# A hybrid decoder layer: half boundaries on other banks, two diagonal score steps in one slot, casting copies moved off the sequence change, later loads at the start, and the last weights in a slot of their own

## The chip, the cores and the metric

One Trainium2 chip, all 8 cores. Each core computes two of the sixteen sequences and exchanges nothing with the others. The metric is the device time of the slowest core in microseconds. Some executions fall into a slower state, in which one die or both get a lower TensorE clock (in the slow run of `b_bank` 0.88 to 0.89 on cores 0 to 3 and 0.99 on the others, in one of `spread_model` 0.81 to 0.83 on all eight); they are named slow below and never compared with fast ones. Spans of single cores come from the profiled execution of each kernel.

## The reference, cut to what matters

```python
BATCH, SEQ, D_MODEL, D_FF = 16, 2048, 1024, 2816
# per layer (depth 1):
x = x + 0.5 * rms(swiglu(rms(x, g1), w_gate, w_up, w_down), g2)      # FFN 1
x = x + rms(hybrid_mixer(rms(x, g3)), g4)                            # attention
x = x + 0.5 * rms(swiglu(rms(x, g5), w_gate2, w_up2, w_down2), g6)   # FFN 2
# hybrid_mixer: one input projection (1024 -> 3072); 4 differential heads
# (two 64-wide score maps each, causal, dense, values 128 wide) beside
# 8 dilated heads (three window patterns); one output projection (1024 -> 1024)
```

## The kernel before

The program is one stream of nodes. A planner orders them for each engine at build time, with estimated durations; the chip then runs that fixed order, each engine waiting on semaphores. An FFN half is 1024 tokens of one sequence: a gate/up pass (22 jobs) and a down pass (8 jobs). Each job is done in seven products over sums of blocks instead of eight over the blocks themselves; banks `y` and `y + 1` take over the first product, which is needed twice, and accumulate others on top.

```python
DMA_RATE = 280.0          # what the planner assumes of transfers: GB/s, us, us
DMA_LAT = 2.4
DMA_AHEAD = 5.0
...
# gate/up pass
    y = (2, 6)[ji % 2]
    pb = (0, 4, y, 0, 4, y, y)[n]                   # bank of product n of job ji
    ...
    if n == 0:
        copy(two(y), [B_ps[y], B_ps[y + 1]], 0)     # banks 0,1 -> y,y+1 on ScalarE
...
# down pass
    y = 2 + ji % 2
    pb = (0, 4, y, 0, 4, y, y)[n]
...
# ffn_half: the normalisation of the half before is finished in banks 6 and 7
for k, p in enumerate(pend):
    p(6 + k, g.clock + 3.0 + 0.3 * k)
```

The second FFN's weights are cast from 32 to 16 bits by 30 copies from memory to memory, which run during attention. Attention goes through 16 units (8 head groups of two sequences). In the first step of each unit two copies are released, by the last TensorE node before them; four semaphores rotate, so at most four are under way:

```python
def cast_chunk(i, pace):
    ...
    g.dma(POOL, [(d, s_)], [pace], [b, B_ctr[i % 4]], kb * 1.15, track=B_ctr[i % 4])
...
for w, (s, u) in enumerate(units):
    ...
        if first:
            first = False
            ...                      # pace: written by the last TensorE node
            for c in range(2):
                if 2 * w + c < NF + NKC:
                    cast_chunk(2 * w + c, pace)
```

The units from the last of the first sequence to the first of the second are called the sequence change here. A differential score step computes one block of 128 keys against 512 queries, for two maps; on the diagonal only the later 512, 384, 256 or 128 queries count:

```python
def scores(Q, kt, box):
    mp = kt - 4 * Q
    c0 = max(mp, 0) * 128
    si = nxt("S", 2)                                # one of two pairs of banks
    ...                                             # 2 matmuls of 512 - c0 columns, 64 rows
    g.op([(ACT, a_ps(n), act_(P[:, :, c0:TT], sp[:, :, c0:TT], AF.Exp, ...))], bs, [bP])
...
for kt in range(4 * Q + 4):
    ...                                             # scores, then values, of step kt
```

The start loads the first input tile and weights, then the tile after and the next half's as soon as their buffers allow. At the very end, the second half of the last down pass takes its last weights through the ring of slots, and every square of the last statistics is added on VectorE before one product with ones on TensorE.

The softmax here doesn't subtract the row's maximum and nothing guards it: scores larger than these inputs give would overflow.

## Time and profile before

| | us |
|---|---|
| median of 3 runs (one of them slow, 2854.82) | 2540.53 |
| fast runs | 2539.59, 2540.53 |
| TensorE busy on core 4 (span 2536.5) | 2437.88 |

The view of the cores lists span and mean granted clock. Cores 6 and 7 were granted a lower clock in this execution and lose it in the first stage (189 and 192 us), the others lie within 15 us of each other:

```profile
core 2: 2524.9 us, clock 0.994
...
core 4: 2536.5 us, clock 0.993
...
core 7: 2562.1 us, clock 0.983
```

TensorE is busy nearly all the time, so the rows of engines say little. To see where time goes I divide each core's span at fixed matmuls of the program: the first down projection, the first value projection of attention, the first and the 256th matmul of the output projection (between them lies the sequence change), the first matmul of FFN 2, the last gate/up matmul and the last matmul of all. All stage tables below are worked out from the traces in this way and give the median over the 8 cores. For the kernel before:

| start | rest of FFN 1 | attention, first half | sequence change | attention, rest | FFN 2 to the last gate/up | last down pass | tail |
|---|---|---|---|---|---|---|---|
| 169.7 | 673.2 | 380.6 | 85.8 | 392.0 | 745.8 | 74.8 | 9.8 |

### The profile page before, as it was taken

How to read it: one execution, taken by the hardware profiler on the slowest of the kernel's cores; microseconds unless marked ns; L12 is line 12 of the kernel's file. 1: busy time of each engine (PE TensorE's matmuls, PEld its weight loads, DVE VectorE, ACT ScalarE, POOL GpSimd, SP SyncE). 2: the span in 40 equal slices, each digit the busy share in tenths (PEclk: the TensorE clock that was granted, in tenths of full speed). 3: DMA queues.
4: the chain of work that ended last, by engine and by line, in shares of the span. 5: the costliest groups of instructions: out<-in, count | busy, mean ns of one | idle time of the engine just before them, and what ended most of it. 6: DMA issues, size and time to landing. Idle time of an engine off the chain costs nothing.

```text
span 2562.1 us, 49653 instructions; the slowest of 8 cores (2521.7 to 2562.1 us)
## 1 busy us (share of the span) xinstructions
PE 2465.2 (96%) x16526; PEld 1289.4 (50%) x16526; DVE 1854.5 (72%) x3172; ACT 1398.7 (55%) x2070; POOL 421.7 (16%) x483
## 2 busy tenths in 40 slices
PE   6999999999999999999989999999999999999997
PEld 4444444444444556656546666544444444444466
DVE  6656796797797774556687455499777967967974
ACT  4433654554554477777677677775434544534433
POOL 1110220121131221111122110013102101201302
PEclk9889999999999999999999999999999999999999
DMA  7565586496596993425569352258245444534634
GB/s 172 112 132 132 146 167 135 141 185 115 148 203 117 221 207 70 64 55 122 118 152 219 84 100 40 58 171 255 90 135 168 144 132 156 167 122 137 201 124 143
DMA packets 154969, 356.15 MB, mean 139 GB/s; under 512 B 28416, under 2 KB 39296, under 8 KB 154112
## 3 DMA queue, kind: packets, MB, share of 16 engines
q1 hardware_dynamic: 129872, 260.89, 33.7%
q0 software_dynamic: 24848, 92.09, 22.5%
q8 instruction: 138, 2.26, 0.4%
q14 instruction: 111, 0.91, 0.1%
HBM read 381.84 MB, written 80.48 MB: 180 GB/s over the span
## 4 chain that ended last, share of the span: by engine, by line
PE 89%; DVE 3%; ACT 2%; issue 2%; DMA 2%; POOL 0%; DVEq 0%; ACTq 0%; POOLq 0%; SPq 0%
PE ps L942 41%; PE ps L1011 21%; PE ps L1147 8%; PE ps L1278 5%; PE ps L1109 4%; PE ps L1184 3%; PE ps L1243 3%; PE ps L1407 2%; ACT M L641 2%; DVE M L638 1%; PE ps L1370 1%; DMA M<-xT 1%; DMA M<-x 1%; DVE M L770 0%; DVE M L704 0%
## 5 line engine op out<-in xcount | busy, mean ns | idle before, releaser
L641 ACT ACTIVATE M<-ps 128x1024 bf16<-128x1024 f32 (+8 forms) x1191 | 880.7, 777 | 578.2 <-PE ps L942 174.8
L942 PE MATMUL ps<-M 128*128 128x512 f16 (+1 forms) x5096 | 1101.1, 379 | 22.9 <-ACT ps L641 10.6
L638 DVE TENSOR_TENSOR M<-M 128x1024 f16<-128x1024 f16 (+10 forms) x1602 | 953.1, 629 | 222.2 <-ACT M L641 95.5
L942 PEld LDWEIGHTS ps<-M 128*128 128x128 f16 x5096 | 503.7, 99 | 614.8 <-issue 105.4
L641 ACT ACTIVATE M<-M 128x512 f32<-128x512 f32 (+4 forms) x648 | 385.9, 618 | 490.9 <-DVE M L638 417.8
L1011 PE MATMUL ps<-M 128*128 128x512 f16 (+2 forms) x2926 | 547.6, 348 | 4.0 <-DMA M<-cdn 2.5
L638 POOL TENSOR_TENSOR M<-M 128x512 f32<-128x512 f32 (+3 forms) x248 | 305.9, 1240 | 1277.7 <-DVE M L770 570.5
L1011 PEld LDWEIGHTS ps<-M 128*128 128x128 f16 x2926 | 276.1, 99 | 269.3 <-issue 21.9
L638 DVE TENSOR_TENSOR M<-ps,M 128x1024 f32<-128x1024 f32 (+5 forms) x322 | 304.2, 948 | 129.5 <-PE ps L1011 72.6
L1147 PE MATMUL ps<-M 128*128 128x512 f16 x1024 | 263.0, 379 | 4.7 <-DVE M L1121 1.8
L638 DVE TENSOR_TENSOR M<-M,ps 128x512 f16<-128x512 f32 (+1 forms) x182 | 120.9, 665 | 64.7 <-PE ps L942 44.8
L1278 PE MATMUL ps<-M 128*128 128x129 bf16 x2176 | 162.8, 221 | 1.9 <-DVE M L638 1.7
L1278 PEld LDWEIGHTS ps<-M 128*128 128x128 bf16 x2176 | 134.2, 98 | 47.9 <-issue 26.3
L1109 PE MATMUL ps<-M 128*128 128x128 f16 x2048 | 141.3, 219 | 8.3 <-DVE M L1307 2.4
L704 DVE SCALAR_TENSOR_TENSOR M<-M,gains 128x512 f16<-128x512 f32 x192 | 134.9, 748 | 16.8 <-ACT M L641 16.6
L641 ACT ACTIVATE ps<-ps 128x1024 f32<-128x1024 f32 (+3 forms) x129 | 108.2, 839 | 62.7 <-PE ps L1011 45.1
L770 DVE SCALAR_TENSOR_TENSOR M<-M,gains 128x512 f16<-128x512 f16 x176 | 140.0, 815 | 1.6 <-ACT M L641 1.5
L1109 PEld LDWEIGHTS ps<-M 128*128 128x128 f16 x2048 | 119.8, 98 | 27.1 <-issue 22.5
L1147 PEld LDWEIGHTS ps<-M 128*128 128x128 f16 x1024 | 86.1, 97 | 86.5 <-issue 23.7
L1184 PE MATMUL ps<-M 128*128 128x512 f16 x512 | 119.5, 382 | 8.5 <-DVE M L1094 5.8
L1094 DVE CAST M<-ps 128x512 bf16<-128x512 f32 (+1 forms) x97 | 66.9, 689 | 76.1 <-PE ps L1147 56.2
L1243 PE MATMUL ps<-M 64*128 64x512 bf16 (+3 forms) x640 | 96.3, 352 | 10.3 <-ACT M L641 10.0
(54 smaller groups left out, 750.1 us busy)
## 6 DMA issues: line engine op xcount, KB each, us to landing
M<-x SPq DMA_DIRECT2D x128, 512.0 KB, 6.5
M<-cgu SPq DMA_DIRECT2D x88, 512.0 KB, 4.2
M<-xT SPq DMA_DIRECT2D x64, 512.0 KB, 8.1
x<-M SPq DMA_DIRECT2D x64, 512.0 KB, 7.2
M<-wgu POOLq DMA_DIRECT2D x58, 512.0 KB, 8.4
M<-cdn SPq DMA_DIRECT2D x38, 704.0 KB, 4.3
M<-wd POOLq DMA_DIRECT2D x32, 704.0 KB, 8.0
M<-c1g SPq DMA_DIRECT2D x30, 512.0 KB, 4.2
```

What stands on the lines that cost most here:

```text
L638: return lambda e: e.tensor_tensor(o, a, b, op)
L641: return lambda e: e.activation(o, i, f, **k)
L704: g.op([(DVE, v_stt(512), lambda e, o=o, kc=kc: e.scalar_tensor_tensor(o, halves(xt.ap(kc)), gains[:, gcol + kc:gcol + kc + 1], halves(rst ...
L770: g.op([(DVE, v_stt(512), lambda e, y=y, d=d: e.scalar_tensor_tensor(y, y, gains[:, gcol + d:gcol + d + 1], rst[ri], ALU.mult, ALU.mult))] ...
L942: g.pe([(lambda e, gg=gg, kc=kc, pb=pb, src=src, piece=piece, n=n, w=w, cs=cs: e.matmul(bank(pb + gg)[:, 0:w], src[:, gg * 512 + kc * 128: ...
L1011: g.pe([(lambda e, k=k, b=pb, src=src, piece=piece, n=n, c0=c0, W_=W_: e.matmul(bank(b)[:, 0:W_], src[:, k * 128:(k + 1) * 128], H[piece][ ...
L1094: g.op([(DVE, vc or v_ps(n), lambda e: e.tensor_copy(o, i)), (ACT, a_ps(n), act_(o, i, AF.Copy))], rd, wr, pen=EVPEN)
L1109: g.pe([(lambda e, kc=kc: e.matmul(bank(pb)[:, tq * 128:(tq + 1) * 128], xn[:, kc, t * 128:(t + 1) * 128], wap[:, kc * 128:(kc + 1) * 128] ...
L1147: g.pe([(lambda e, kc=kc: e.matmul(bank(pb), wap[:, kc * 128:(kc + 1) * 128], xn[:, kc, ts(tt)], start=(kc == 0), stop=(kc == NKC - 1)), [ ...
L1184: g.pe([(lambda e, k=k: e.matmul(bank(pb), wap[:, k * 128:(k + 1) * 128], mixT[k][:, ts(tt)], start=(k == 0), stop=(k == NKC - 1)), [wb, B ...
L1243: g.pe([(lambda e, m=m: e.matmul(sp[:, m, c0:TT], KT[i][64 * m:64 * m + 64, kt * 128:(kt + 1) * 128], QT[i][64 * m:64 * m + 64, Q * TT + c ...
L1278: ops.append((lambda e, a_ap=a_ap, m=m, uq=uq, first=first: e.matmul(a_ap, P[:, m, uq * 128:(uq + 1) * 128], Vt[i][:, kt, 0:129], start=(k ...
```

## The change

Five parts. The half boundaries of the FFN change banks, so that the first copy of a half needs no bank that the down pass still holds. Diagonal score steps 1 and 3 share a slot. Casting copies avoid the first unit and the sequence change, and others take up to three. The start gates some loads, chains others behind the second input tile, and gives the planner slower transfers. At the end the last weights get their own slot and the last squares go straight to TensorE. The matmuls multiply as much as before.

```diff
-DMA_RATE = 280.0
-DMA_LAT = 2.4
-DMA_AHEAD = 5.0
+DMA_RATE = 260.0
+DMA_LAT = 3.0
+DMA_AHEAD = 8.0
...
+OWN = 2
+NXH = 2
+CHAIN = 2
...
+CASTS = (0, 2, 3, 2, 3, 2, 2, 0, 0, 2, 3, 3, 3, 3, 2, 0)
...
-                y = (2, 6)[ji % 2]
+                y = (6, 2)[ji % 2]
...
+                        elif lead and l < lead + CHAIN:
+                            b = x1[0]
+                            aft = [[b.buf(3)], [b.buf(5)]] if l == lead else [[W[l - 1][k][1]] for k in (0, 6)]
+                            W[l] = load_blocks(fi, "g", l, after=aft)
...
+                def parts(Q, kt):
+                    r = [(kt, max(kt - 4 * Q, 0) * 128, max(kt - 4 * Q, 0) * 128)]
+                    if kt == 4 * Q + 1:
+                        r.append((kt + 2, 384, 0))
+                    return r
...
-                    for kt in range(4 * Q + 4):
+                    for kt in range(4 * Q + 3):
...
-                        for c in range(2):
-                            if 2 * w + c < NF + NKC:
-                                cast_chunk(2 * w + c, pace)
+                        for c in range(CASTS[w]):
+                            cast_chunk(sum(CASTS[:w]) + c, pace)
...
-                p(6 + k, g.clock + 3.0 + 0.3 * k)
+                p(2 + k, g.clock + 3.0 + 0.3 * k)
...
-                                 c + 20.0 + 20 * tl)
+                                 c + 20.0 + 20 * tl, after=[B_H[0][NXH]] if (s, fi, h) == (0, 0, 0) else ())
...
+                wx = (o_RS, rbuf("wx", o_RS, 5632))
...
-                sa, sb_ = Stat(3, 256), Stat(2, 256)
+                sa = Stat(3, 256, own=[(ssum[i], B_ssum[i]) for i in range(OWN)])
+                sb_ = Stat(2, 256, own=[(sq[i], B_sq[i]) for i in range(OWN)])
...
-                               (2, (1,), 0, 128, fa), (1, (1,), 128, 128, fb), (2, (1,), 128, 128, fb)], keep, {3: W[3]})
+                               (2, (1,), 0, 128, fa), (1, (1,), 128, 128, fb), (2, (1,), 128, 128, fb)], keep, {3: W[3]},
+                          {2: lambda kind, j: wx if j == 0 else ring_slot(kind, j)})
```

## The prediction

Where a cut is marked, statements that no trace of this case shows were taken out; the figures left between the cuts were read from the trace of the kernel before. The sum came to 26 us.

> **What bounds the kernel now.** I read the table of cores first, then the busy time of each engine in stretches of 50 us, then who the tensor engine waited for, then the timeline around its longest waits. The page is of core 7, whose clock was granted lower (0.983); I read core 4 instead, which spans 2536.5 us at a clock of 0.993, close to the timed median of 2540.5 us. From the stretches of core 4 (columns: stretch, its length, busy us of each engine with instruction counts, granted clock, DMA share, GB/s):
>
> ```profile
> 0.00:50.00 50.00, 27.79 (x185) 18.66 (x185) 29.19 (x56) 21.52 (x38) 5.84 (x13) 0.90 0.78 169
> 50.00:100.00 50.00, 45.03 (x289) 27.81 (x290) 40.51 (x80) 27.46 (x51) 9.83 (x14) 1.00 0.69 121
> ...
> 850.00:900.00 50.00, 47.20 (x514) 30.94 (x513) 42.22 (x82) 35.36 (x55) 12.75 (x16) 1.00 0.86 168
> ...
> 1300.00:1350.00 50.00, 41.19 (x429) 25.34 (x427) 39.50 (x77) 33.31 (x51) 16.47 (x20) 0.97 0.87 200
> ...
> 1600.00:1650.00 50.00, 43.94 (x398) 24.23 (x397) 28.56 (x60) 37.67 (x53) 2.33 (x2) 0.93 0.13 42
> ...
> 2500.00:2550.00 50.00, 21.75 (x326) 20.10 (x324) 14.31 (x43) 11.69 (x37) 9.62 (x14) 0.85 0.33 108
> ```
>
> The sum of that table gives TensorE 2437.88 us busy of 2536.5, so all idle time together is 98.6 us. No other engine is near: VectorE is busy 1855 us, ScalarE 1397. The change removes no matrix multiplication, so it can gain only from those 98.6 us, from matmuls run at a lower clock, and from small gaps inside busy stretches. By stage the idle is: 27 us before 100, about 9 in the first FFN from 100 to 845, 46 in attention (845 to 1706), 5 in the second FFN, and some 15 after 2500. The waits of TensorE on core 4 (us in total, times, longest):
>
> ```profile
> PE ps L942 <- ACT ps L641: 11.3, 9, 1.9
> PE ps L731 <- DVE M L638: 11.0, 1, 11.0
> PE ps L1243 <- ACT M L641: 10.0, 18, 1.1
> ...
> PE ps L1184 <- DVE M L1094: 6.6, 5, 5.3
> ...
> PE ps L1011 <- DMA M<-cdn: 2.0, 1, 2.0
> ```
>
> The first is repeated at the FFN half boundaries, the fourth is one event at the sequence change, the fifth is the late weights of the end. The second is the wait for the first input tile; nothing in the change touches it. The timeline of one half boundary:
>
> ```profile
> 238.95 1.89 PE L942 MATMUL ps<-M 128*128 128x512 f16 x8
> ...
> 243.36 0.60 ACT L641 ACTIVATE M<-ps 128x512 f16<-128x512 f32 x1 [3.17 <-PE ps L1011]
> 244.11 1.15 ACT L641 ACTIVATE M<-M 128x512 bf16<-128x512 f16 x2
> ...
> 245.16 1.00 ACT L641 ACTIVATE ps<-ps 128x1024 f32<-128x1024 f32 x1
> ...
> 246.31 1.02 PE L942 MATMUL ps<-M 128*128 128x512 f16 x4 [1.37 <-ACT ps L641]
> ```
>
> The reader is to see that the first products of the new half were done at 240.8, but the copy of them from banks 0 and 1 to banks 2 and 3 started only at 245.16: bank 3 was the last accumulator of the down pass, freed by the 243.36 copy, and two squares ran in between. TensorE then stood 1.37 us. The sequence change, first from the chain of work in order of time, then the timeline:
>
> ```profile
> 1286.37 15.77 DMA M<-x
> ```
>
> ```profile
> 1279.87 0.98 POOL L147 DMA_DIRECT2D cgu<-wgu  x2 [12.82 <-PE ps L1278]
> ...
> 1302.35 3.25 POOL L638 TENSOR_TENSOR M<-M 128x512 f32<-128x512 f32 x3 [9.26 <-DMA M<-x]
> ...
> 1305.70 0.69 DVE L1311 TENSOR_REDUCE sml<-M 128x4 f32<-128x512 f32 x1 [5.75 <-POOL M L638]
> ...
> 1308.53 3.38 PE L1184 MATMUL ps<-M 128*128 128x512 f16 x8 [5.30 <-DVE M L1094]
> ```
>
> Two casting copies start at 1279.87; the residual load issued at 1286.37 takes 15.77 us; GpSimd's adds wait for it, VectorE's reduction waits for a GpSimd product queued behind them, the evacuation queued behind that is late, and TensorE stands 5.30 us.
>
> [...] 15.77 us against a median of 6.3 for these loads. [...] after 5.30 us of idle, 8 matmuls took 3.38 us against 1.89 for the same 8 elsewhere. [...] The groups by shape give 1022 ns for 1024 columns, 809 for 768 and 379 for 256, so fusing the last two saves 809 + 379 - 1022 = 166 ns.
>
> **The change part by part.**
>
> (1) Half boundaries. The FFN's jobs start on banks 6 and 7 instead of 2 and 3, which the down pass does not use, and the deferred statistics move to 2 and 3. The copy can then follow its matmuls at once, behind one matmul group of 1.7 us. Between 240 and 840 and between 1730 and 2450 the waits table gives three such waits each, 4.1 us each: 8.2 us in all. The last job of most halves now ends on banks 6 and 7 and meets no bank of the down pass. I take 8.
>
> (2) Casting copies. None in the first unit and in the units either side of the sequence change; others take 3. It removes the 5.30 us wait and the slow restart (3.38 - 1.89 = 1.5): 6.8. At the attention's start two waits of 0.86 and 0.81 us stand beside the first copies (issued at 872.8): I give 1. The same 30 copies remain and all still precede the second FFN. I take 7 in all, with something lost to other loads left there.
>
> (3) Diagonal scores. Steps 1 and 3 (384 and 128 columns) share one slot, so each query block has one step fewer: 4 blocks x 4 units x 2 sequences = 32 fewer of 320. Multiplications are as many. What goes is a change to 64-row mode and back. In the timeline at 1610.21, two 512-column matmuls (0.216 us each, from 126.91 us for 588 in the chain) end at 1610.64, the score group starts at 1610.73, its two pairs end at 1611.16 and the next starts at 1611.27: 0.09 + 0.11 = 0.2 us for a group. I counted 211 score groups on the timeline, 1.52 steps in each; 288 steps make 190, so 21 x 0.2 = 4.2 us. ScalarE saves 0.166 us in 8 steps, 1.3 us, beside other work. Against it: the shared step holds its banks through two activations in three heads of four, so the next one waits longer. I take 3.5.
>
> (4) Start. Loads for the next half wait until the third job has finished, the fourth and fifth weights wait for the second input tile, and the planner's transfer model is slower (260 instead of 280, latency 3.0 instead of 2.4). This should stop ScalarE from standing in program order behind squares whose input has not arrived: the 1.9 us at 65.31 and part of the 2.98 us at 38.02 and of the waits of about 1.4 nearby. I take 3.5.
>
> (5) End. The last weights have a slot of their own: 2.01 us of wait, and the restart at 2509.51 (11 matmuls of 128 columns in 1.23 us against 0.77 for 11 at 2523.80) gives 0.5. The last two squares go to TensorE directly: the final sum stood 1.92 us behind VectorE; two additions drop out, but only the last, 0.36 us with its hand-over, and its wait on the addition before are on the chain, say 0.8. VectorE may share the last additions without penalty (0.37 us each against GpSimd's 0.7): say 0.7. I take 4.
>
> Sum: 8 + 7 + 3.5 + 3.5 + 4 = 26 us.
>
> **The rivals.** First, a new static order. The program is ordered by a planner at build time; the altered transfer model and slots shift thousands of instructions, and some of the 46 us of attention idle comes back elsewhere. For it: its waits are many and small (18 on score banks, 10.0 us). Against it: the planner had these same rules before. It would make 2520 to 2530. Second, the sequence change may stay bound by transfers: output weights and residual tiles load there as well (DMA share 0.87 from 1300 to 1350), so only half of the 6.8 us returns, and units with three copies instead of two see late loads: 2520. Third, the fewer steps and the calmer transfers help more of the attention than I count, perhaps 10 us of its 46: 2503. Fourth, ScalarE becomes the bound in attention; it is busy there about three quarters of the time, and the change takes a little from it, so I give this little.
>
> **Range and chances.** 2540.5 - 26 = 2514.5; I say 2515, 1.0% less. Eight in ten: 2503 (all parts whole, attention a little better) to 2529 (boundaries and end alone). Faster by over 2% means below 2489.7, 51 us of the 98.6, while some 11 at the start and much of the last 15 can't go: 3%. Slower by over 2% needs a serious new wait: 1%. Within 2%: 96%.
>
> **What would show it.** (1) The waits of about 1.4 us on the copies at the six half boundaries are gone. (2) The 5.30 us wait is gone and residual loads there land in 6 to 9 us. (3) 288 score steps, some 190 groups, and attention shorter by 10 us or so with (2). (4) Idle before 100 us falls from 27 to about 23. (5) No wait for the last weights; the stretch after 2500 shorter by 4. The prediction fails if idle in attention grows elsewhere by over 10 us, or if the FFN loses less than 6 us.

## More of the kernel before

The sequence change has two values: 88 to 91 us on cores 0, 3, 4 and 7, 82 to 84 on the others. Attention as a whole takes 858.7 in the median.

## The result, and the profile after

| | before | after |
|---|---|---|
| median of 4 runs each, same chip | 2540.06 (one slow) | 2527.45 (2526.12 to 2528.03) |
| ratio of fast runs, 95% interval | | 0.9953 (0.9933 to 0.9972) |

A ratio here is the mean time of one kernel's fast runs over that of the other's of the same rounds, so it is not quite the ratio of the medians quoted. The gain is some 12 us where 25 were predicted. By stage, in us:

| | start | FFN 1 rest | att. first half | seq. change | att. rest | FFN 2 | last down | tail | attention, whole |
|---|---|---|---|---|---|---|---|---|---|
| before | 169.7 | 673.2 | 380.6 | 85.8 | 392.0 | 745.8 | 74.8 | 9.8 | 858.7 |
| after | 170.6 | 667.7 | 383.1 | 83.5 | 394.2 | 738.9 | 70.3 | 9.7 | 860.4 |
| predicted change | -3.5 | -4.1 | with the rest | about -7 | -10.5 in all of attention | -4.1 | -4 with the tail | | -10.5 |

Both FFNs and the end gained more than was said or as much; the start and attention, 14 us of the predicted 26, gained nothing. The cores of the changed kernel tell more. The view of the cores, after:

```profile
core 0: 2523.2 us, clock 0.990
core 1: 2524.6 us, clock 0.990
core 2: 2508.7 us, clock 0.993
```

Core 2 is 15 us shorter than its neighbours with the same program, and its mean clock is higher. Whatever costs the others 15 us is not in the order of instructions. The waits of TensorE on core 0 after (us in total, times, longest; L752 is the first statistics, which wait for the first input tile, L968 the gate/up products, L1135 the value projection, L1173 the query and key projection):

```profile
PE ps L752 <- DVE M L650: 13.0, 1, 13.0
...
PE ps L1173 <- DVE M L1120: 6.1, 4, 2.9
PE ps L1135 <- issue: 5.8, 2, 4.7
...
PE ps L1173 <- issue: 2.5, 1, 2.5
```

Two things are to be seen. The waits of the gate/up products on ScalarE's copies, 11.3 us on core 4 before, have left the top of the list, and between 240 and 835 us, and again between 1730 and 2440, this view lists no wait at all. And a new kind has come: "issue", a wait for nothing that the profile shows. Before, all waits of that kind came to 0 to 1.9 us on a core; after, to 8.3, 10.6, 0.6, 9.7, 3.4, 6.1, 6.1 and 8.6 us on cores 0 to 7. The core with 0.6 is the short one. (In later kernels that keep the old placing of the copies, two at a time, these waits come to up to 4.1 us on a core, in `a_nocast` to 6.0: they are not new in kind, but in size.)

The half boundary that the prediction showed, in the timeline of core 0 after:

```profile
239.40 1.89 PE L968 MATMUL ps<-M 128*128 128x512 f16 x8
...
241.13 2.54 PE L1037 MATMUL ps<-M 128*128 128x512 f16 x11
241.39 1.01 ACT L653 ACTIVATE ps<-ps 128x1024 f32<-128x1024 f32 x1 [0.74 <-PE ps L968]
...
243.50 3.83 PE L968 MATMUL ps<-M 128*128 128x512 f16 x17
```

The copy from bank to bank starts 0.1 us after its matmuls end, not 4 us later, and TensorE goes from one group to the next without a bracket, that is without a wait.

The stretches of 50 us, core 0 after (columns as in the prediction):

```profile
0.00:50.00 50.00, 25.16 (x156) 16.61 (x157) 29.32 (x56) 21.66 (x37) 5.14 (x12) 0.84 0.71 148
50.00:100.00 50.00, 49.56 (x319) 31.83 (x318) 37.77 (x74) 26.35 (x49) 9.56 (x14) 0.95 0.74 141
...
1300.00:1350.00 50.00, 44.94 (x494) 29.42 (x493) 44.29 (x82) 36.19 (x53) 15.11 (x17) 0.98 0.83 207
...
1600.00:1650.00 50.00, 45.02 (x420) 24.94 (x420) 30.95 (x64) 39.12 (x55) 2.33 (x2) 0.97 0.19 54
2500.00:2550.00 50.00, 11.47 (x189) 10.63 (x186) 10.90 (x31) 6.67 (x21) 9.25 (x13) 0.91 0.16 45
```

TensorE of this core is busy 25.16 + 49.56 = 74.7 us of the first 100, where core 4 of the kernel before was busy 27.79 + 45.03 = 72.8, so that idle time seems to have fallen by 1.9. Yet it had done 156 + 319 = 475 matmuls by 100 us, and before 185 + 289 = 474. The busy time that seems gained is slower time: the granted clock is 0.84 and 0.95 where it was 0.90 and 1.00. This is why busy time alone can't be read as progress. These are two different cores, too, and core 4, with 27.2, had the most idle time of the eight before: the median of the cores is 24.9 us of idle in the first 100 in both kernels. The sequence change (1300 to 1350) has 494 matmuls in 50 us instead of 429: that part of the change did what it was for. On all cores: before, TensorE stood 6.3, 3.8, 5.3 and 4.4 us there on cores 0, 3, 4 and 7, and the residual loads around it landed in 4.8 to 16.8 us; after, no core stands over 2 us before the output projection there, and these loads land in 3.6 to 6.1 us.

At the end, the chain of work of core 4 before went through a transfer of 8.56 us to the last weights; that of core 0 after shows one unbroken piece of down projection in its place:

```profile
2500.81 8.56 DMA M<-cdn
```

```profile
2484.39 17.93 PE ps L1037 x242
```

**The new waits.** The longest of them in the timeline of core 0, GpSimd and TensorE (L147 is the helper that issues copies):

```profile
1474.52 1.01 POOL L147 DMA_DIRECT2D cdn<-wd  x2 [1.41 <-PE ps L1135]
...
1479.95 0.55 POOL L147 DMA_DIRECT2D cdn<-wd  x1
...
1485.57 0.40 PE L1135 MATMUL ps<-M 128*128 128x128 f16 x4
...
1490.67 1.46 PE L1135 MATMUL ps<-M 128*128 128x128 f16 x12 [4.70 <-issue]
```

A burst of three casting copies is issued, and some 6 us after the last one TensorE stops for 4.70 us in the middle of one group of sixteen matmuls, which need nothing new. Core 2 at the same instruction:

```profile
1482.73 0.84 PE L1135 MATMUL ps<-M 128*128 128x128 f16 x12 [0.59 <-issue]
```

So the place in the program is the same and the length differs by core. The transfers of core 0 after, from 1466.06 to 1487.6 us, as the view of the queues lists them (packets, MB, share of the 16 engines; then KB and us to landing for an issue):

```profile
q0 software_dynamic: 661, 2.95, 94.3%
q14 instruction: 1, 0.01, 0.1%
...
cdn<-wd POOLq DMA_DIRECT2D x3, 704.0 KB, 15.2
M<-win POOLq DMA_DIRECT2D x3, 256.0 KB, 4.7
```

(Queue q0 carries the copies, `cdn<-wd`, and loads of projection weights, `M<-win`: three of 704 KB and three of 256 KB make up its 2.95 MB. The last of these loads was issued at 1472.58, before the copies, and these loads land in 4.7 us.)

Queue q8, which the profile also calls "instruction", is not in the list. Its packets in the trace are of 16,384 bytes each; they end at 1450.3, 1457.3 and 1466.06, then there is none until one runs from 1487.61 to 1489.16, and TensorE resumes 1.5 us after that one ends. In the 20 us between, TensorE executed 231 matmuls, 230 weight loads and 23 semaphore instructions and then stopped. The packets carry no engine's name. What ties them to TensorE is a count: there are 138 of them on core 0, and TensorE has 35,429 instructions (as many matmuls counted as weight loads, since 38 records are missing), 256.7 for each. Between the ends of two packets it has 257 in the median, and half of the intervals lie between 210 and 290; the counts of the other engines scatter more (half of them between 27 and 42 on ScalarE, 27 and 63 on VectorE). During the stall the copies' queue holds 97% of the engines. All eighteen waits of this kind above 1.2 us in the attention of the changed kernel, over the eight cores, have the same shape: a packet of q8 ends 0.7 to 1.7 us before TensorE resumes, and in sixteen of them the copies' queue holds 92 to 100% of the engines (in the other two 27 and 52%).

The longest packet of the copies took 3.2 to 5.9 us in these stalls, the packet of q8 0.9 to 2.0. The trace shows this coincidence; what made the packet of q8 late, it does not show.

This stall is paid twice, since a stretch at half clock goes with it. The windows of core 0 after, from the stall on, and of a longer window for comparison with a later experiment:

```profile
1470.00:1500.00 30.00, 24.26 (x283) 17.52 (x282) 12.14 (x33) 16.85 (x24) 5.20 (x8) 0.89 0.84 120
...
1491.00:1500.00 9.00, 8.83 (x84) 6.13 (x83) 3.52 (x12) 5.18 (x7) 1.60 (x2) 0.77 0.59 97
```

From 1491 to 1500 TensorE is busy again, at a mean clock of 0.77; the clock records of the trace have half clock from 1488.4 to 1495.2. Over the whole of attention, TensorE of the changed kernel spends 18.3 us at half clock in the mean of the cores, before 9.4.

### The profile page after: what moved, and what is told of

It reads as the page before. It is cut to its first block, busy times and chain, and to the rows that moved or that the text cites. A ratio compares the mean times of both kernels' runs of the same rounds, so it can differ in the third digit from the quotient of the medians.

```text
span 2524.6 us, 49509 instructions; the slowest of 8 cores (2508.7 to 2524.6 us)
## 1 busy us (share of the span) xinstructions
PE 2438.3 (97%) x16530; PEld 1289.9 (51%) x16530; DVE 1853.5 (73%) x3187; ACT 1426.2 (56%) x2080; POOL 408.4 (16%) x470
## 4 chain that ended last, share of the span: by engine, by line
PE 91%; DVE 3%; issue 2%; ACT 2%; DMA 1%; POOL 0%; DVEq 0%; ACTq 0%; POOLq 0%; SPq 0%
PE ps L968 42%; PE ps L1037 21%; PE ps L1173 9%; PE ps L1319 5%; PE ps L1135 4%; PE ps L1210 3%; PE ps L1277 3%; PE ps L1448 2%; ACT M L653 2%; PE ps L1411 1%; DVE M L650 1%; DMA M<-x 0%; DVE M L725 0%; DMA M<-xT 0%; PE ps L715 0%
## 5 line engine op out<-in xcount | busy, mean ns | idle before, releaser
L653 ACT ACTIVATE M<-ps 128x1024 bf16<-128x1024 f32 (+9 forms) x1179 | 879.0, 782 | 567.3 <-PE ps L1037 171.3
L968 PE MATMUL ps<-M 128*128 128x512 f16 (+1 forms) x5096 | 1077.0, 373 | 11.3 <-DVE M L650 4.8
L650 DVE TENSOR_TENSOR M<-M 128x512 bf16<-128x512 bf16 (+10 forms) x1608 | 932.0, 613 | 189.3 <-ACT M L653 87.7
L968 PEld LDWEIGHTS ps<-M 128*128 128x128 f16 x5096 | 499.6, 98 | 583.4 <-issue 17.7
L1037 PE MATMUL ps<-M 128*128 128x512 f16 (+2 forms) x2926 | 540.5, 345 | 1.2 <-DVE M L650 0.6
L650 POOL TENSOR_TENSOR M<-M 128x512 f32<-128x512 f32 (+3 forms) x238 | 292.5, 1236 | 1320.7 <-DVE M L791 638.8
L1173 PE MATMUL ps<-M 128*128 128x512 f16 x1024 | 261.1, 381 | 10.5 <-DVE M L1120 6.1
L791 DVE SCALAR_TENSOR_TENSOR M<-M,gains 128x512 f16<-128x512 f16 x176 | 152.7, 886 | 3.5 <-ACT M L653 3.5
L1135 PE MATMUL ps<-M 128*128 128x128 f16 x2048 | 144.1, 221 | 8.7 <-issue 6.9
L1173 PEld LDWEIGHTS ps<-M 128*128 128x128 f16 x1024 | 87.1, 98 | 100.6 <-issue 33.0
L1135 PEld LDWEIGHTS ps<-M 128*128 128x128 f16 x2048 | 121.4, 98 | 28.8 <-issue 24.5
```

Of the source, the lines that this page charges most:

```text
L650: return lambda e: e.tensor_tensor(o, a, b, op)
L653: return lambda e: e.activation(o, i, f, **k)
L791: g.op([(DVE, v_stt(512), lambda e, y=y, d=d: e.scalar_tensor_tensor(y, y, gains[:, gcol + d:gcol + d + 1], rst[ri], ALU.mult, ALU.mult))] ...
L968: g.pe([(lambda e, gg=gg, kc=kc, pb=pb, src=src, piece=piece, n=n, w=w, cs=cs: e.matmul(bank(pb + gg)[:, 0:w], src[:, gg * 512 + kc * 128: ...
L1037: g.pe([(lambda e, k=k, b=pb, src=src, piece=piece, n=n, c0=c0, W_=W_: e.matmul(bank(b)[:, 0:W_], src[:, k * 128:(k + 1) * 128], H[piece][ ...
L1135: g.pe([(lambda e, kc=kc: e.matmul(bank(pb)[:, tq * 128:(tq + 1) * 128], xn[:, kc, t * 128:(t + 1) * 128], wap[:, kc * 128:(kc + 1) * 128] ...
```

## The experiments

**Theory S (starvation):** bursts of up to three copies, with which q0 holds 94.3% of the transfer engines in the list above, are what makes TensorE stand in the waits called "issue" (4.70 us there); take the bursts away and keep everything else, and the predicted gain comes. **Rival O (order):** the planner's new static order moved the waits about, and no single part is at fault. **Rival C (copies):** moving copies out of the sequence change is worth nothing, since they hurt wherever they run. Further, each part alone, to size it. All fourteen runs (of thirteen kernels, one of them twice) gave correct results. Runs of one heading stood on the same chip and share the runs of the kernel before, except that the last two stood on a chip of their own, with runs of the kernel before of their own (median of the fast ones 2538.3). Some runs that count as fast have two cores of one die at a clock near 0.98 and are some 20 us longer, as 2559.47 and 2562.8 of the kernel before on the first chip; they widen the intervals, so the times of the undisturbed runs are given too. Passages that no trace shows are cut from the expectations, too, with the cut marked. Rival B of `b_cast` and theory A of `a_spread` and `a_burst` stand for theory S; rival B of `a_spread` puts the waits down to the program, and rival B of `a_nocast` holds that bursts of three cost in such waits what keeping copies away from the sequence change gains.

### Each part alone

The four kernels are the kernel before with one part of the diff.

`b_bank`, the banks only:

```diff
-                y = (2, 6)[ji % 2]
+                y = (6, 2)[ji % 2]
-                p(6 + k, g.clock + 3.0 + 0.3 * k)
+                p(2 + k, g.clock + 3.0 + 0.3 * k)
```

> The kernel before with the bank part alone (first job of an FFN half on banks 6 and 7, deferred statistics in 2 and 3). Theory A, the waits for the banks were the whole cost of the half boundaries: the six waits of about 1.4 us on the copies are gone, the two FFN stages are shorter by 10 to 13 us together, the time falls by 9 to 13 us (ratio 0.995 to 0.9965). Rival B, the FFN gain in the changed kernel comes from the new transfer model of the planner and not from the banks: the waits stay or others take their place, the FFN stages are shorter by less than 4 us.

Measured: 2526.09, 2526.3 and 2527.14 us (one more run slow), ratio 0.9924 (0.9859 to 0.9989). FFN 1 takes 668.1 instead of 673.2, FFN 2 739.4 instead of 745.8: 11.5 us, nothing lost elsewhere (attention 857.3 against 858.7). A gate/up pass from the boundary on took 131.5 us on core 2 of the kernel before and 129.9 here in FFN 1, 131.8 to 132.1 and 129.9 in FFN 2. So each boundary gave 1.5 to 2.2 us where the list of waits had 1.37. Theory A holds: the median of the fast runs falls from 2538.7 to 2526.3. This one part alone is worth about the whole gain of the change.

`b_cast`, the copies only:

```diff
-                        for c in range(2):
-                            if 2 * w + c < NF + NKC:
-                                cast_chunk(2 * w + c, pace)
+                        for c in range(CASTS[w]):
+                            cast_chunk(sum(CASTS[:w]) + c, pace)
```

> The kernel before with the new placing of the casting copies alone (none in units 0, 7, 8 and 15, up to three at once in others). Theory A, as predicted: the wait of 5.3 us at the sequence change is gone on all cores, time down by 5 to 7 us. Rival B, [...] waits put down to issue grow from at most 2 us to 4 to 10 us on most cores, and the time stays within 3 us of before.

Measured: fast runs 2541.0, 2542.77 and 2564.57 us, ratio 1.0014 (0.9934 to 1.0095). The sequence change is 82.3 to 83.6 us on every core, against 82 to 91 before: the wait is gone. The first half of attention is 2.9 us longer (383.5), and waits of the kind "issue" are 6.4, 1.0, 0.5, 2.6, 0, 5.5, 0.4 and 5.4 us. So the part gives and takes: in all nothing, or 2 to 4 us lost in the two undisturbed runs (before 2537.6 to 2539.7). Theory A's 5 to 7 us did not come; rival B's size of the waits came on three cores of eight. The waits of core 0 here show it beside the boundary waits that this kernel still has:

```profile
PE ps L974 <- ACT ps L659: 9.5, 8, 1.4
...
PE ps L1141 <- issue: 6.0, 2, 3.6
```

`b_score`, the shared slot of two diagonal steps only (the `parts` hunk of the diff):

```diff
+                    if kt == 4 * Q + 1:
+                        r.append((kt + 2, 384, 0))
-                    for kt in range(4 * Q + 4):
+                    for kt in range(4 * Q + 3):
```

> The kernel before with the shared slot of the diagonal score steps alone. Theory A, as predicted: fewer changes of row mode, attention shorter by 3 to 5 us. Rival B, the true number of score groups falls only by some 10 [...], so that attention changes by less than 2 us before the effects of another order, which may be several us either way.

Measured: 2530.78 to 2537.95 us, ratio 0.9961 (0.9905 to 1.0017). The first half of attention takes 375.4, 5.2 less, but the sequence change 88.9: six of eight cores are in the long mode now. So the whole of attention is only 1.2 us shorter in the median (857.5), as rival B said, and not the 3 to 5 of theory A. The best core's attention takes 847.3 us against 853.0. The part is worth more than the median tells, and the transfers of the sequence change hide it: on core 2, in the long mode, TensorE stands 4.45 us for an evacuation by VectorE, which had stood 4.67 us for a residual load; core 7, in the short one, has neither wait.

`b_end`, the end only (own slot, own squares, no penalty on VectorE):

```diff
+                wx = (o_RS, rbuf("wx", o_RS, 5632))
+                sa = Stat(3, 256, own=[(ssum[i], B_ssum[i]) for i in range(OWN)])
```

> The kernel before with the end part alone (last weights in their own slot, last squares summed by TensorE, last additions shared). As predicted: the wait for the last weights is gone, the last down pass shorter by 3 to 5 us, everything else as before, time down by 3 to 5 us. Rival: the end is bound by its last stores and gains less than 1 us.

Measured: 2534.14 to 2538.88 us (one run slow), ratio 0.9961 (0.9895 to 1.0028). The last down pass takes 70.2 us on all eight cores; before it took 72 to 77. The tail after it stays at 9.7. From the last down matmul to the last sum on TensorE it is 1.5 us, before 1.9; the rest of the gain is the wait for weights, which differed by core. This is as expected, in the stage; the times alone would not tell.

### The copies in the changed kernel

Three kernels are the changed kernel with only the copies' placing altered, and a fourth is the kernel before with the start alone.

`a_spread`, the changed kernel with each copy at its own share of the unit instead of all at the first step; same list of copies by unit:

```diff
-                    if first:
-                        first = False
-                        ...
-                        for c in range(CASTS[w]):
-                            cast_chunk(sum(CASTS[:w]) + c, pace)
+                    while ncast < CASTS[w] and nstep >= ncast * sum(k == w for k, x in steps) // CASTS[w]:
+                        pn = next(n for n in reversed(g.nodes) if n.alts[0][0] == PE)
+                        pace = Buf("pace%d_%d" % (w, ncast))
+                        ...                                  # pn writes pace
+                        cast_chunk(sum(CASTS[:w]) + ncast, pace)
+                        ncast += 1
+                    nstep += 1
```

> The changed kernel with the same casting copies in the same units, but one at a time, evenly over the unit, instead of up to three at its start; hardly any other instruction moves. Theory A, [...] the waits put down to issue fall from 3 to 10 us on seven of eight cores to less than 3 us, the slowest core comes near the best core of the changed kernel (2508.7 us), time 2511 to 2519 us. Rival B, [...] issue waits stay at 3 to 10 us and the time at 2525 to 2529.

Measured: 2512.29 and 2515.4 us in fast runs, two more runs slow (2678.9 and 2678.16), so no ratio was computed; the spans of the cores are 2507.9 to 2513.9. Waits of the kind "issue": 0.2, 0, 0, 0, 0.4, 0, 0.7, 0. Attention 851.6 in the median and 854.8 on the slowest core, where the changed kernel has 860.4 and 868.1. One edit that moves copies in time takes the new waits away and some 13 us. On core 2 the two traces have the same sequence of operations and shapes on TensorE, ScalarE and VectorE, 21,797 instructions, and differ in 42 places on GpSimd and SyncE, so rival O, the order, can't be what cost the time. In the mean of the cores TensorE is idle 38.4 us in attention instead of 44.3 and at half clock for 10.2 us instead of 18.3. The stretch of core 0 in which the changed kernel stalled:

```profile
1470.00:1500.00 30.00, 28.77 (x340) 19.34 (x337) 15.51 (x47) 21.54 (x30) 4.26 (x5) 1.00 0.65 118
```

`a_burst`, the other direction: the same copies in half as many bursts:

```diff
-CASTS = (0, 2, 3, 2, 3, 2, 2, 0, 0, 2, 3, 3, 3, 3, 2, 0)
+CASTS = (0, 0, 5, 0, 5, 0, 4, 0, 0, 0, 5, 0, 6, 0, 5, 0)
```

> The changed kernel with the casting copies gathered in bursts of four to six in half as many units: the suspected cost doubled. Theory A, [...] issue waits of 4 to 10 us at the start of each of those units, 15 to 40 us in all on each core, time 2535 to 2560 us. Rival B: issue waits as in the changed kernel, time 2524 to 2531.

Measured: 2529.05 to 2532.25 us, ratio 0.9965 (0.9948 to 0.9983). Waits of the kind "issue": 15.4, 4.7, 9.0, 14.2, 10.7, 12.6, 13.7 and 5.9 us, attention 866.1. With more copies in a burst there are more stalls, 86 us in all over the eight cores against 53, and 3 to 4 us more time; the longest single one, 4.4 us, is no longer than before (4.7). Theory A had said more, 15 to 40 us on each core and at least 2535 us: the direction came, the size did not. This edit also moves ScalarE's and VectorE's order, so it is a weaker test than `a_spread`. On core 0:

```profile
PE ps L1135 <- issue: 8.0, 2, 4.1
```

`a_nocast`, the changed kernel with the old two copies in each unit:

```diff
-CASTS = (0, 2, 3, 2, 3, 2, 2, 0, 0, 2, 3, 3, 3, 3, 2, 0)
+CASTS = (2,) * 15 + (0,)
```

> The changed kernel with the copies placed as before, two at the start of each of the first fifteen units. Theory A, as predicted: the wait of several us at the sequence change comes back on about half of the cores, time 3 to 7 us longer than the changed kernel (2530 to 2534). Rival B, [...] issue waits fall below 2.5 us on all cores and the time is within 3 us of the changed kernel.

Measured: fast runs 2516.52 and 2518.82 us (two slow), ratio 0.9913 (0.9889 to 0.9937). "Issue" waits 1.7 to 6.0 us, attention 850.7 in the median and 858.9 on the slowest core, sequence change 84.8. Neither expectation came, as both put the time near the changed kernel's or above it: leaving the part out would have been better by 10 us than putting it in. The copies one at a time are about 3 us better still by the time; the median of attention is the same within 1 us (850.7 here, 851.6 in `a_spread`), and only the slowest core is shorter.

`b_startmodel`, the kernel before with gated loads, the chain, and the planner's new estimates of transfers (the edit in short):

```diff
-DMA_RATE, DMA_LAT, DMA_AHEAD = 280.0, 2.4, 5.0
+DMA_RATE, DMA_LAT, DMA_AHEAD = 260.0, 3.0, 8.0
+NXH = 2
+CHAIN = 2
```

> The kernel before with the later loads of the start and the slower transfer model of the planner alone. Theory A, as predicted: the first 170 us get 3 to 4 us shorter. Rival B, the waits are gathered instead of removed, TensorE's clock drops to half for some 10 us there and the first 170 us stay within 1.5 us of before. The model also reorders the rest; the FFN boundaries keep their six waits of 1.4 us either way.

Measured: 2536.56, 2537.91 and 2539.58 us (one slow), ratio 0.9993 (0.9974 to 1.0013); the first stage takes 170.8, 1.1 more than before. The 3 to 4 us of theory A did not come.

### Spacing on the kernel before, and the start in its parts

`b_spread`, the kernel before with the new list of copies, one at a time (the edit of `a_spread`):

> The kernel before with the changed unit list of casting copies, but each copy placed at its own share of the unit instead of in a burst at the unit's first step; nothing else of the change. Starvation theory (bursts of three copies hold the transfer engines [...]): the stalls called issue fall under 1 us per core (6.4 at most with the same list in bursts), the sequence change stays at 82 to 84 us on every core, the first attention half stays near 380 us, and the time is 4 to 8 us under before, near 2533. Rival (moving copies out of the sequence change is worth nothing, and the change of the first attention half came from the copies' load whatever their spacing): stalls stay at 3 us or more on some cores and the time is within 2 us of before, as with the bursts.

Measured: fast runs 2533.16, 2534.51, 2534.61, 2538.46 and 2558.71, ratio 0.9993 (0.9946 to 1.0039). The trace has what theory S said: "issue" waits of 0.5 us at most, the sequence change at 82.8, the first half of attention at 381.0. Attention takes 854.8 in the median and 857.4 on the slowest core, before 858.7 and 863.6. The moved copies are worth 4 us of attention, not 7, once they do no harm.

`spread_again`, the kernel of `a_spread` in more rounds:

> The changed kernel with the copies one at a time, once more and in more rounds, since two of its four runs were slow and no ratio came of it. Starvation theory: 2510 to 2517 us in fast runs, ratio 0.988 to 0.992, issue stalls under 1 us on every core. Rival (the first look was a lucky one): within 4 us of the changed kernel's 2527.

Measured: four fast runs of 2512.84 to 2515.07 us, two slow; ratio 0.9889 (0.9854 to 0.9924). "Issue" waits 1.4 us at most, on one core above the 1 us that I had named.

`spread_oldstart`, as that but with the old start and the old estimates (the edit put together in short):

```diff
-NXH = 2, CHAIN = 2, DMA_RATE = 260.0, DMA_LAT = 3.0, DMA_AHEAD = 8.0
+(no gate, no chain), DMA_RATE = 280.0, DMA_LAT = 2.4, DMA_AHEAD = 5.0
```

> As the run with copies one at a time, but with the old start of the program (loads of the first pass ungated, chain of normalisation scalings as before) and the old transfer estimates of the planner. If the start part costs what it seemed to (about 1 us from the begin to the first down-projection), this is 0.5 to 2 us faster than the copies-one-at-a-time kernel and the first stage is 169.5 to 170 us. Rival (the start part is worth the 3.5 us that were predicted and other parts hid it): 2 to 4 us slower, the first stage 172 or more.

Measured: six runs, 2508.48 to 2513.66 us, median 2511.81, none of them slow; ratio 0.9881 (0.9853 to 0.9909). First stage 169.2. It is faster than the kernel before and the changed kernel; from `spread_again` (median of fast runs 2513.1) it differs by less than either's runs scatter. Its core 0 in the window in which the changed kernel stalled, and its queues from 1466 to 1500 us:

```profile
1470.00:1500.00 30.00, 29.34 (x349) 20.02 (x346) 14.51 (x43) 21.50 (x31) 4.25 (x5) 1.00 0.47 102
```

```profile
q0 software_dynamic: 516, 2.20, 40.1%
...
q8 instruction: 3, 0.05, 0.6%
...
cdn<-wd POOLq DMA_DIRECT2D x2, 704.0 KB, 7.1
```

349 matmuls in 30 us at a full clock, against 283 at 0.89. Packets of q8 come, three in these 34 us, and a copy lands in 7.1 us instead of 15.2.

`b_start`, the kernel before with gate and chain, but the old estimates:

> The kernel before with the start part alone (gated loads of the first pass and scalings chained), planner estimates as before. The prediction said 3.5 us less in the first stage. What the changed kernel's trace suggests instead: waits gathered into one place and half-clock windows of 10 to 14 us between 41 and 54 us from the span's start, first stage 170 to 171 us against 169.7, time within 2 us of before. Rival (start part is good, planner estimates spoil it): first stage 166 to 167 us, time 2 to 4 us under before.

Measured: 2534.85 to 2541.27 us (one slow), ratio 0.9978 (0.9942 to 1.0013), first stage 168.3. My theory of the start fell here: I had held the gate responsible for the late start, and alone it gains 1.4 us. The rival, that the estimates spoil it, came nearer. So the square was completed on the kernel with copies one at a time.

`spread_newstart`, gate and chain without the estimates:

> Copies one at a time, gated loads and chained scalings of the start kept, planner estimates as before. If the estimates and not the gating spoil the start: first stage near 168 us in the median of the cores (169.2 with neither, 171.1 with both), time 2509 to 2513. Rival (gating and estimates are both noise): first stage 169 to 170, time within 1 us of the run with neither, 2512.

Measured: fast runs 2508.82, 2512.04 and 2515.77 us, ratio 0.9895 (0.9881 to 0.991), first stage 167.7. Not to be told from `spread_oldstart` by the time.

`spread_model`, the estimates without gate and chain:

> Copies one at a time, old start, new planner estimates. If the estimates spoil the start by themselves: first stage 171 to 172 us, time 2513 to 2517. Rival (they only hurt together with the gating): first stage 169 to 169.5, time 2511 to 2513.

Measured: fast runs 2512.99, 2513.23, 2514.69, 2514.87 and 2533.69 us, three slow; ratio 0.9921 (0.9892 to 0.995). First stage 170.2, under the 171 that I had expected.

| first stage, us | old estimates | new estimates |
|---|---|---|
| before: no gate | 169.7 | |
| before: gate and chain | 168.3 | 170.8 |
| copies one at a time: no gate | 169.2 | 170.2 |
| copies one at a time: gate and chain | 167.7 | 171.1 (170.1 in the first look) |

By this table the gate gains 1.4 to 1.5 us with the old estimates and nothing with the new; the new estimates cost 1.0 to 3.4. How far to trust it: the same stage with the old start and estimates measures 168.6 to 170.3 in the seven kernels that have them, and two profiles of one kernel differ by 1.0 (170.1 and 171.1). So a cost of the estimates of about 1 us is shown, as no kernel with them is under 170.1 and only one without is over 169.7; the gain of the gate is barely clear of the scatter. The first 50 us of core 4 in `spread_oldstart` and of core 0 in `spread_model` tell which it is:

```profile
0.00:50.00 50.00, 28.13 (x193) 19.54 (x193) 29.92 (x57) 22.84 (x40) 5.81 (x13) 0.93 0.79 169
```

```profile
0.00:50.00 50.00, 25.79 (x156) 17.01 (x157) 29.17 (x56) 22.29 (x38) 5.14 (x12) 0.85 0.82 175
```

All profiled starts with the new estimates have 145 to 160 matmuls there and a clock of 0.82 to 0.86, all with the old ones 172 to 194 and 0.86 or more. The order that the planner makes of the slower transfers leaves TensorE more waits close together, around 36 to 49 us in the changed kernel (on core 4 of 1.29, 2.45, 1.62 and 1.05 us), and half clock goes with them: 13.7 us from 40.8 on that core, where the kernel before had 3.4 us from 38.4.

## Why the prediction was right or wrong, point by point

**The step that failed is (2), casting copies: "I take 7 in all, with something lost to other loads left there."** The wait of 5.30 us and its slow restart did go, on every core, as the signs (2) had said. Two terms were wrong. The first is its size: the wait was there on core 4 and three others, not on all, so the list of one core stood for all eight; alone and without bursts the move gives 4 us of attention (`b_spread`). (Of the two waits at the attention's start, worth 1 us in the sum, the first ended at 870.55, 2.2 us before the copies beside it were issued.) The second is what was left out: to keep 30 copies, other units take three at once, and the prediction allowed for late loads there (its second rival) but not for the waits called "issue". This costs 9 to 10 us of attention in the median of the cores (860.4 against 851.6 and 850.3) and 13 to 16 on the slowest (868.1 against 854.8 and 852.5), and the slowest core sets the time. With bursts the part takes 10 us in this kernel instead of giving 7: `a_nocast` runs in 2516.5 to 2518.8, the changed kernel in 2527. The test is `a_spread`: same copies, same units, same parts, other spacing, and the new waits and 13 us are gone; `a_burst` turns the same screw the other way. The prediction's own alarm, idle in attention growing elsewhere by over 10 us, did not ring in the median of the cores (42.1 to 45.1 us): part of the loss is half clock, which isn't idle (18.3 us in attention in the mean of the cores, before 9.4).

**(4), start: "I take 3.5" fell too.** It put gate and chain and the planner's estimates into one term and gave all of them the waits that they might remove. Gate and chain give about 1.4, the estimates take that and more; together the first stage is 0.9 us later. Sign (4) said idle before 100 us would fall from 27 to about 23. On core 4, from which the 27 was read, it did fall, to 24.2, but its time at half clock there grew, and its first stage is only 0.8 us shorter; in the median of the cores idle did not fall (24.9 in both). The sign was ill chosen, since idle is not progress and core 4 was not typical.

**(1), half boundaries: right in mechanism, too small.** The sign came: no wait at a boundary is left. 8 was the term, 11.5 (`b_bank`) to 12.4 (changed kernel) is the measure. What the list of waits gave as 1.37 a boundary was 1.5 in FFN 1 and 1.9 to 2.2 in FFN 2, 10.6 for the six, and the first pass of FFN 2 gained 0.4 to 1.0 us in the median as well. What these extra pieces are, below the size of a listed wait, I did not resolve.

**(3), diagonal scores: right in sign, wrong in its working.** It said 21 fewer score groups (211 to 190); counted in the traces in the same way on both sides it is 200 before and 190 after. All score groups taken, TensorE goes from matmuls of 128 rows to matmuls of 64 and back 13 fewer times (586 changes on core 4 before, 560 on core 2 after). On both, a 512-column matmul is followed by the next after 312 ns at a change and after 216 otherwise (medians in attention), so a change costs about 0.1 us, as the prediction read it, and the 26 changes are worth some 2.5 us. Yet the part gave more than the 3.5 of the prediction: attention takes 848.5 in `spread_oldstart` and 850.0 in `spread_newstart`, 854.8 in `b_spread`, which has the same copies and estimates without the shared slot, so 5 to 6 us; and 5.2 in the first half of attention by itself in `b_score`. Where the other 2 to 4 us come from (fewer turns of the two pairs of banks, less ScalarE work) is open; no run separates them.

**(5), end: the sum right, its split not.** 4 was said, 4.5 came. The tail did not shrink (9.8 to 9.7) although two terms of 0.8 and 0.7 were set for it. The statistics gave 0.4, and the wait for weights some 4 instead of 2.5, as other cores waited longer than core 4's list said.

**The rivals.** The first, a new static order, was given 2520 to 2530, and the time did fall there, but not through it: with the same new order on TensorE, ScalarE and VectorE it is 2514 (`a_spread`). The second, transfers, was the right suspect named for the wrong victim. The third, more help in attention than counted, did not come: without bursts attention is 10.2 us shorter (`spread_oldstart`), the sum had 10.5. Without bursts and without the start part the gain is 27 us (2539.2 to 2511.8, medians of the fast runs on one chip), where the other four terms of the prediction came to 22.5 and all five to 26. That the sum would nearly have fitted is in part luck: 8 stood for some 12, 7 for 4, 3.5 for 5 or 6 and 3.5 for nothing.

**A slip in its reading.** The idle time by stage adds up to 102 us, not to the 98.6 above it; the trace of core 4 has 5.9 in the first FFN, 43.6 in attention and 7.2 in the second FFN. No term of the sum was built on these shares.

What stays open: why the stalls come at the same places but differ by a factor of ten between cores; why the same copies stall more in the changed kernel than in the kernel before (53 us over eight cores against 22 in `b_cast` with bursts, 29 in `a_nocast` against 7 with two at a time), so that the part costs 10 us in one and about nothing in the other; and what makes the packets of q8 late: that the bursts do is inferred from the order in time and from the spacing experiments, and how they would is not shown.

## What to carry to other kernels

When background transfers are moved away from a place where they hurt, spread them, and look at the waits called "issue", which name no buffer: here they came to 53 us over the eight cores with bursts of up to three, and to 1.3 with the same copies one at a time (`a_spread`). Compare all cores of one program before reading one of them: a core that is shorter with the same order of instructions points at something outside the order (core 2 here, by 15 us). And read busy time together with the clock and the count of matmuls, since time at half clock looks like work: here 74.7 us against 72.8 in the first 100, for 475 matmuls against 474.
